# Folding the attention weights of a decoder trunk ahead of its values: more places for raw loads, split weights in idle slots, another order and another pacing

## The chip, the cores and the metric

The kernel runs on one core of one Trainium2 chip. The metric is the device time of one execution in microseconds; the time before is the median of three runs. Beside it there is one profiled execution, whose trace gives the start, the length and the releaser of every instruction on the engines: PE (matrix products, with PEld for the weight loads), DVE (elementwise), ACT (elementwise with scaling and functions), POOL and SP. DMAs are issued from the queues of SP, ACT and POOL.

## The reference

One layer of a decoder trunk over x, 2048 tokens of 1024 channels, all in float32, with 256 memory tokens:

```
h = rmsnorm(x);  q, k, v, g, u = split(h @ w_in)
y = concat(silu(g) * head_rmsnorm(retention(q, k, v)), pool_mixer(u))
x = x + y @ w_out
x = x + cross_attn(rmsnorm(x), rmsnorm(mem), xa_wq, xa_wkv, xa_wo)
x = x + conv_glu_ffn(rmsnorm(x), w_up, conv_w, conv_b, w_down)
out = rmsnorm(x)
```

The cross-attention has four heads of 256 channels. Its scores are (h wq)(mem wk)^T and its output is p (mem wv) wo, so for each head the products wq (mem wk)^T and (mem wv) wo can be made once, before any token is seen. The pooling mixer's per-group weight, its scale and its part of w_out can be multiplied together in the same way.

## The kernel before

**Numbers.** Every float32 operand is split in two parts, a high part rounded to the fast format of PE and a low part with the rest. `split` (line 256 for ACT's high part, line 240 or 248 for DVE's low part) makes both, and `passes` (lines 268 to 270) runs three products per pair: high by high, high by low, low by high. A tile of weights thus goes through a load on SP's queue into a raw place, a split by ACT and DVE into a pair place, and then PE.

**Stages.** The kernel first folds weights (`folded_weights`), then handles the tokens in two halves of 1024: values, head projections with retention and pooling, the mixing with w_out, attention, the output of attention; then the MLP of both halves with a seven-product scheme of block matrices (`rounds`, `run`).

**The folding stage.** `folded_weights` is a generator of 28 units and a closing step, in an order written out by hand. K units (`keys`, 8) and V units (`memory_values`, 8) multiply the memory by a column tile of `wkv`; M units (`score_weights`, one per head, two tiles of `wqT` each) make the score weights and store them in `Md`; O units (`output_weights`, two tiles of `wo` each) make the output weights and store them in `VWd`; W units (`pool_weights`) make `WPd`. Results leave PSUM by ACT into slots of `T` and are stored by DMAs issued from ACT's queue (`keep`, line 519). Between the units the caller, in the main part of the kernel, places other work at fixed unit numbers: eight x tiles (`load_x_wide`, lines 611 to 618: load, split into the slots of X, square, add to a running total), the rope tables (`stored_tables`), the norm of x, the four tiles of value weights (`value_weights`, line 691), and steps of `weight_sums`.

**Places.** `raws` are five places of 128 x 1024 for raw loads: three in `R`, two tiles `S`. In the folding stage two of them hold the memory at first and one holds the running total of x's squares. `wides` are five places for a pair of split parts of 1024: one in `Q`, four in a version of tile `Z` that is replaced by another version after the stage. G holds the split x in its slots 0 to 15 (two per tile of x) and the split memory, keys and values in the slots from 16 on; E has four more slots. `new_raw` and `wide` take the place that was freed longest ago; a load or a split into it waits until its readers are done.

**Order.** The instructions are traced in program order and then put in order by a scheduler with modelled times; calls such as `keep_in_program_order` and `issue_after` hold some of them. Each engine and each queue then runs its own in that order.

**Weight sums.** `weight_sums` prepares block sums for the seven-product schemes (`Ad` for the heads, `Ud` and `Dd` for the MLP) with DMAs from DRAM to DRAM on POOL's queue, some of them accumulating. Each step begins with a tiny ACT instruction (line 942) and a POOL copy (line 943), and issues the next DMAs of up to four jobs; `spacing[0]` says after how many calls the next step comes. There are 52 steps.

**After the fold.** `values` makes the values of the first half with the four tiles of value weights, while `quarter_sums` (line 1510 for its loads) prepares block sums of x, some of them in Z, for the head projections, in which each of 56 items calls `weight_sums`.

Of the kernel before, what the change touches and what calls it, by code (L numbers as in the profile page):

```python
# [8 lines left out]
F32 = mybir.dt.float32  # L9
F32R = mybir.dt.float32r  # L10
I32 = mybir.dt.int32
AF = mybir.ActivationFunctionType
# [8 lines left out]
T = 1024  # L21
SUB = 512
NB = SEQ // T
NS = T // SUB
# [112 lines left out]
def trunk(ctx, tc, xT, memT, pos, w_qkgu, w_v, wkv, wqT, wo, wout_r, wout_p, poolT, w_up, w_dn, vecs, consts, outT):  # L137
# [24 lines left out]
    def new_z(dtype):  # L162
        return Arena(cp.tile([P, 8 * T + 4 * EDGE], dtype, tag="Z", name=nm("Z")), 0, 8, T)

    TT = Arena(cp.tile([P, TEMPS * TW], F32, tag="T", name="T"), 0, TEMPS, TW)
    R = cp.tile([P, 3 * T], F32, tag="R", name="R")
    Q = cp.tile([P, 3 * T], F32R, tag="Q", name="Q")
# [254 lines left out]
    def folded_weights():  # L422

        mp = B.take(4)
# [2 lines left out]
        kk, vv = B.take(4), B.take(4)  # L427
        kp4, vp4 = (r.r.rearrange("p (n i m) -> p n i m", i=2, m=NMEM) for r in (kk, vv))
        own = [prs.take() for _ in range(2)]
        zr = new_z(F32R).t  # L430
        wides = Places([(Q, 0)] + [(zr, 2 * i * T) for i in range(4)], 2 * T)
        memory, first = [raws.take() for _ in range(2)], new_raw()
        for q in range(4):
            to = memory[q // 2].f[:, q % 2 * SUB : (q % 2 + 1) * SUB].rearrange("p (k m) -> p k m", m=NMEM)
# [75 lines left out]
        def memory_values(n):  # L510

            project(KT + n)
            if n % 2:
                split(bank[0].rearrange("p (n m) -> p n m", n=2), vp4[:, n - 1 : n + 1, 0], vp4[:, n - 1 : n + 1, 1])
            if n == KT - 1:
                mp.free()

        def keep(dst, t, n):
            act.dma_start(dst, t.f[:, :SUB].rearrange("p (n c) -> p n c", n=n))
            t.free()  # L520

        def tiles4(d, nh, k):
            return d[4 * nh : 4 * nh + 4, :, k, :].rearrange("n p c -> p n c")
# [1 line left out]
        def score_weights(h):  # L525

            dp = [row_pair(wqT[(2 * h + dt) * P : (2 * h + dt + 1) * P, :]) for dt in range(2)]
            for k2 in range(KT // 2):
                ps = mmps()
                for j in range(2):  # L530
                    for dt in range(2):
                        k = 2 * k2 + j
                        passes(ps[:, j * NMEM : (j + 1) * NMEM], [r[:, k * P : (k + 1) * P] for r in dp[dt]],
                               (kp4[:, 2 * h + dt, 0], kp4[:, 2 * h + dt, 1]), dt == 0, dt == 1)
                t = TT.take()
                for j in range(2):
                    k = 2 * k2 + j
                    act.activation(t.f[:, j * NMEM : (j + 1) * NMEM], ps[:, j * NMEM : (j + 1) * NMEM], AF.Identity, scale=xag[:, k : k + 1])
                keep(Md[h // 2, 2 * k2 : 2 * k2 + 2, :, (h % 2) * NMEM : (h % 2 + 1) * NMEM].rearrange("k p m -> p k m"), t, 2)
            if h == HEADS - 1:  # L540
                kk.free()

        def output_weights(h):

            dp = [row_pair(wo[(2 * h + dt) * P : (2 * h + dt + 1) * P, :]) for dt in range(2)]
            for nh in range(2):
                for mt in range(2):
                    ps = mmps()
                    for dt in range(2):
                        lh = [vp4[:, 2 * h + dt, i, mt * P : (mt + 1) * P] for i in range(2)]  # L550
                        passes(ps, lh, [r[:, nh * SUB : (nh + 1) * SUB] for r in dp[dt]], dt == 0, dt == 1)
                    t = TT.take()
                    act.activation(t.f[:, :SUB], ps, AF.Identity, scale=rn[:, mt : mt + 1])
                    keep(tiles4(VWd, nh, 2 * h + mt), t, 4)
            if h == HEADS - 1:
                vv.free()
# [3 lines left out]
        def pool_weights(g):  # L560

            if g == 0:
                raw = new_raw()
                r3 = raw[:, :SUB].rearrange("p (g c) -> p g c", g=4)
                sp.dma_start(r3, poolT.rearrange("g p c -> p g c"))
                pw = prs.take()
                tt(dve, r3, r3, bcast(pscale, P), ALU.mult)
                split(raw[:, :SUB], pw.r[:, :SUB], pw.r[:, SUB:])
                pool_pair.append(pw)
            pw = pool_pair[0]  # L570
            u = row_pair(wout_p[g])
            for nh in range(2):
                ps = mmps()
                lh = [pw.r[:, i * SUB + g * P : i * SUB + (g + 1) * P] for i in range(2)]
                passes(ps, lh, [r[:, nh * SUB : (nh + 1) * SUB] for r in u], True, True)
                t = TT.take()
                act.activation(t.f[:, :SUB], ps, AF.Copy)
                keep(tiles4(WPd, nh, g), t, 4)
            if g == 3:
                pw.free()  # L580

        def none_left():
            for r in own:
                r.free()

        K, V, M, O, W = keys, memory_values, score_weights, output_weights, pool_weights
        for f, *a in ((K, 0), (K, 1), (K, 2), (K, 3), (K, 4), (K, 5), (M, 0), (K, 6), (K, 7), (M, 1), (V, 0), (V, 1), (M, 2),
                      (V, 2), (V, 3), (M, 3), (V, 4), (V, 5), (O, 0), (V, 6), (V, 7), (O, 1), (W, 0), (W, 1), (O, 2),
                      (W, 2), (W, 3), (O, 3), (none_left,)):
            f(*a)  # L590
            yield

# [87 lines left out]
    def stored_tables(b):  # L680
        for got in rope_tables(b):
            yield
        minus = TT.take()
        act.activation(minus.f[:, :SUB], got[1].f[:, :SUB], AF.Copy, scale=-1.0)
        for i, r in enumerate((*got, minus)):
            sp.dma_start(rope_d[i], r.f[:, :SUB])
            r.free()
# [222 lines left out]
    def weight_sums():  # L910

        jobs = [((w_qkgu[a], w_qkgu[c]), 0, 4, Ad[p]) for p, (a, c) in enumerate(PAIRS)]
        columns = len(jobs)
        jobs += [((w_up[f], w_up[f + NF]), 0, 4, Ud[f]) for f in range(NF)]
        for at, (k0, n) in enumerate(ROUNDS):
            jobs += [((w_dn[2 * j], w_dn[2 * j + 1]), k0, n, Dd[at, j]) for j in range(KT // 2)]

        def sums(w, k0, n, to):
            a11, a12, a21, a22 = (block(w, i // 2, i % 2, k0, n) for i in range(4))
            d = [to[i][:, : n * P] for i in range(4)]  # L920

            def add(at, a):
                pool.dma_start(d[at], a, accum_op=ALU.add, max_dma_last_dim=2048)

            for i, a in ((2, a21), (0, a11), (1, a11), (3, a12)):
                pool.dma_start(d[i], a, max_dma_last_dim=2048)
            yield
            add(2, a22)
            add(0, a21)
            yield  # L930
            add(1, d[2])
            yield
            add(3, d[1])

        live, jobs, at = [], [sums(*j) for j in jobs], 0
        others = len(jobs) - columns
        while jobs or live:
            if jobs and (len(jobs) <= others or at % 2 == 0):
                live.append(jobs.pop(0))
            at += 1  # L940
            here, there = halo[:, at % 32], halo[:, 40]
            tc.keep_in_program_order(act.activation(here, cs_t[:, P : P + 2], AF.Copy))
            turn = pool.tensor_copy(there, here)
            with tc.issue_after(turn.ins):
                live = [g for g in live if next(g, True) is None]
            for _ in range(spacing[0]):
                yield
# [885 lines left out]
    def norm_tables(s_acc, wide=True, late=False):  # L1833

        rn = rows_norm(s_acc)
        rb, last = [], None
        if wide:
            rb = [TT.take() for _ in range(NS)]
            last = spread(rn, [r.f[:, :SUB] for r in rb], late=late)
        return rn, rb, last  # L1840
# [53 lines left out]

        after(2, step)

    under[0], spacing[0] = weight_sums(), 2
    wv, total, tables0 = [], None, stored_tables(0)
    for n, _ in enumerate(folded_weights()):
        if n in (1, 2, 3, 4):  # L1900
            for _ in range(3):
                next(tables0, None)
        if n == 3:
            total = raws.take()
        if n in (4, 6, 8, 10, 12, 14, 16, 18):
            load_x_wide((n - 4) // 2, total)
        if n == 19:
            normed = norm_tables([total], late=True)
        if n in (18, 21):
            wv.append(value_weights(len(wv), 0))  # L1910
        if n in (24, 25):
            wv.append(value_weights(len(wv), 1))
        if n > 19:
            next(under[0], None)
    Z = new_z(F32)
    slow[0], paced[0] = False, True
    for b in range(NB):

        t1, t2 = (B.arenas[0].take(4) for _ in range(2))
# [21 lines left out]
        finish()  # L1941
        rb = normed[1]
        got.append(v)
        parts = [next(heads)]
        mix = got[1]

# [229 lines left out]
```

## Time and profile before

| | us |
|---|---|
| median of 3 runs | 2487.62 (2484.76 to 2488.1) |
| the profiled execution, device time | 2485.65 |
| its span, first to last instruction | 2483.9 |
| PE busy in it | 2413.6 (97%) |
| DVE / ACT / POOL busy | 1740.3 / 1351.4 / 310.8 |
| DMA moved | 514.67 MB, mean 207 GB/s |

The shares of busy time are means over the whole span. The page's slices of 62 us show PE at six and seven tenths in the first three slices and at nine or more in nearly all later ones, and the clock granted to PE at eight tenths in the first three slices. A row "A <- B: total, times, longest" in the waits says that A stood idle until B ended. A row of the timeline has its start, its length, the engine, the source line, the operation with the tiles, and in brackets the idle time before it with its releaser.

### The profile page before, as it was taken

To read this page: it belongs to the slowest core of one execution; us is meant where nothing else is said; L and a number is where in the kernel's file an instruction comes from. 1 tells how busy PE (TensorE), PEld (TensorE's weight loads), DVE (VectorE), ACT (ScalarE), POOL (GpSimd) and SP (SyncE) were. 2 spreads that over 40 slices of the span, in tenths; PEclk is the share of its full clock that TensorE was granted. 3 is DMA by queue.
4 is the path that set the end of the run, shared out by engine and by line. 5 is a ranking of instruction groups with operands and counts; after the bars stand their busy time and mean duration, and the time that the engine had idled before them with its cause. 6 is when DMAs were issued, how large, how long until landed. Compare 5 with 4: busy or idle time off the path is not lost.

```text
span 2483.9 us, 33353 instructions
## 1 busy us (share of the span) xinstructions
PE 2413.6 (97%) x11232; PEld 2013.5 (81%) x11232; DVE 1740.3 (70%) x2869; ACT 1351.4 (54%) x2457; POOL 310.8 (13%) x484
## 2 busy tenths in 40 slices
PE   6779999999999999999999999999999999999998
PEld 6758887888888888888888888888888888888887
DVE  7536677474676776565688777796768688877876
ACT  5544555343454553433555555665555577666664
POOL 0015565464000000000000000020000000000000
PEclk8889999999999999999999999999999999999999
DMA  6699999999543224446558665665556478768952
GB/s 204 220 279 299 288 284 283 314 294 253 192 148 89 77 77 153 128 153 237 187 178 265 218 191 178 198 218 174 168 167 199 142 228 286 259 180 261 360 186 74
DMA packets 272844, 514.67 MB, mean 207 GB/s; under 512 B 29856, under 2 KB 60960, under 8 KB 272672
## 3 DMA queue, kind: packets, MB, share of 16 engines
q1 hardware_dynamic: 210640, 398.11, 49.3%
q0 software_dynamic: 37376, 86.00, 14.4%
q10 hardware_dynamic: 24656, 28.43, 3.3%
q8 instruction: 88, 1.44, 0.2%
q14 instruction: 84, 0.69, 0.1%
HBM read 410.19 MB, written 188.22 MB: 241 GB/s over the span
## 4 chain that ended last, share of the span: by engine, by line
PE 90%; DMA 4%; DVE 3%; ACT 2%; issue 1%; ACTq 0%; SPq 0%; DVEq 0%
PE mm L268 28%; PE mm L269 28%; PE mm L270 28%; DVE Z L240 1%; DMA R<-wqT 1%; PE aux L268 1%; PE aux L270 1%; PE aux L269 1%; PE aux L762 1%; PE aux L747 1%; PE aux L855 1%; PE aux L736 1%; DMA Z<-rope_d 1%; PE aux L764 1%; ACT Z L256 0%
## 5 line engine op out<-in xcount | busy, mean ns | idle before, releaser
L268 PE MATMUL mm<-G,Q 128*128 128x512 f32 (+1 forms) x1574 | 611.7, 389 | 13.8 <-ACT Q L256 11.6
L270 PE MATMUL mm<-G,Q 128*128 128x512 f32 (+1 forms) x1574 | 608.1, 388 | 0.2 <-DVE Q L240 0.2
L269 PE MATMUL mm<-G,Q 128*128 128x512 f32 (+1 forms) x1446 | 562.0, 389 | 0.2 <-DVE G L248 0.2
L269 PE MATMUL mm<-G,E 128*128 128x512 f32 x1052 | 409.1, 389 | 0.0
L268 PE MATMUL mm<-G,E 128*128 128x512 f32 x1052 | 407.4, 389 | 0.0
L270 PE MATMUL mm<-G,E 128*128 128x512 f32 x1052 | 406.9, 389 | 0.0
L268 PEld LDWEIGHTS mm<-G,Q 128*128 128x128 f32 x1574 | 297.5, 189 | 75.6 <-ACT Q L256 12.4
L270 PEld LDWEIGHTS mm<-G,Q 128*128 128x128 f32 x1574 | 296.9, 189 | 59.7 <-DVE Q L240 0.4
L269 PEld LDWEIGHTS mm<-G,Q 128*128 128x128 f32 x1446 | 273.5, 189 | 54.0 <-DVE G L248 0.4
L240 DVE TENSOR_TENSOR Z<-Z,mm 128x512 f32<-128x512 f32 (+1 forms) x322 | 215.7, 674 | 126.2 <-PE mm L270 122.0
L248 DVE SCALAR_TENSOR_TENSOR Z<-Z,vecs 128x1024 f32<-128x1024 f32 x176 | 224.7, 1280 | 49.6 <-ACT Z L1091 46.2
L270 PEld LDWEIGHTS mm<-G,E 128*128 128x128 f32 x1052 | 197.5, 188 | 41.2
L269 PEld LDWEIGHTS mm<-G,E 128*128 128x128 f32 x1052 | 197.5, 188 | 41.0
L268 PEld LDWEIGHTS mm<-G,E 128*128 128x128 f32 x1052 | 197.4, 188 | 41.0
L1028 ACT ACTIVATE E<-R 128x512 fp32r<-128x512 f32 (+1 forms) x165 | 101.6, 616 | 141.0 <-PE mm L269 135.2
L240 DVE TENSOR_TENSOR Q<-R,Q 128x512 fp32r<-128x512 f32 (+1 forms) x158 | 111.2, 705 | 69.1 <-ACT Q L256 42.2
L240 DVE TENSOR_TENSOR T<-T 128x512 f32<-128x512 f32 (+4 forms) x196 | 134.4, 690 | 20.9 <-ACT T L415 10.5
L240 DVE TENSOR_TENSOR G<-T,G 128x512 fp32r<-128x512 f32 x165 | 110.2, 688 | 30.3 <-ACT G L975 15.7
L1091 ACT ACTIVATE Z<-Z,vecs 128x1024 f32<-128x1024 f32 x88 | 109.2, 1242 | 36.0 <-DVE Z L240 35.1
L975 ACT ACTIVATE G<-T 128x512 fp32r<-128x512 f32 x180 | 108.5, 623 | 35.7 <-DMA T<-Gd 27.7
L1028 ACT ACTIVATE E<-S 128x512 fp32r<-128x512 f32 (+1 forms) x107 | 65.9, 616 | 106.6 <-PE mm L269 105.1
L240 DVE TENSOR_TENSOR E<-R,E 128x512 fp32r<-128x512 f32 (+1 forms) x125 | 83.7, 672 | 41.8 <-ACT E L1028 38.6
(348 smaller groups left out, 4160.3 us busy)
## 6 DMA issues: line engine op xcount, KB each, us to landing
T<-Gd SPq DMA_DIRECT2D x168, 256.0 KB, 4.4
Ud<-w_up POOLq DMA_DIRECT2D x132, 256.0 KB, 10.1
Gd<-Z SPq DMA_DIRECT2D x110, 256.0 KB, 2.8
R<-Ud SPq DMA_DIRECT2D x106, 256.0 KB, 2.7
R<-w_up SPq DMA_DIRECT2D x80, 256.0 KB, 3.1
S<-Ud SPq DMA_DIRECT2D x70, 256.0 KB, 2.8
Gd<-T SPq DMA_DIRECT2D x56, 256.0 KB, 3.3
T<-Xd SPq DMA_DIRECT2D x53, 256.0 KB, 4.2
```

Of the source, the lines that this page charges most:

```text
L240: return eng.tensor_tensor(out=out, in0=a, in1=b, op=op)
L248: return dve.scalar_tensor_tensor(out=out, in0=a, scalar=s, in1=b, op0=op0, op1=op1)
L268: pe.matmul(ps, lh, rh, start=start, stop=False, skip_group_check=more)
L269: pe.matmul(ps, lh, rl, start=False, stop=False, skip_group_check=more)
L270: latest[0] = pe.matmul(ps, ll, rh, start=False, stop=stop, skip_group_check=more)
L736: pe.matmul(col(sc, c), self.ch(k, c), self.ch(q, c), start=True, stop=True)
L747: pe.matmul(col(kv, c), col(self.kn.f, c), self.ch(v, c, h * T), start=True, stop=True)
L762: pe.matmul(col(y, c), col(self.pr.f, c), self.ch(v, c, h * T), start=True, stop=self.cur[c] is None)
L764: pe.matmul(col(y, c), self.ch(q, c), self.cur[c], start=False, stop=True)
L975: one = act.activation(hi, x, AF.Copy, scale=-1.0 if i == 2 else 1.0)
L1028: act.activation(p2[:, 0, :w], self.raw[i].f[:, :w], AF.Copy)
L1091: act.activation(self.c[g].f, a[:, 2:], AF.Identity, bias=cb[:, f : f + 1], scale=cw[2][:, f : f + 1])
```

## The change

It touches the folding stage, what surrounds it, and the pacing of the weight sums.

- `raws` has ten places in the stage: the five of before and five in Z, which is now one float32 tile for the whole kernel. The total's place is taken before the memory's.
- `wides` still begins with five places: Q, two pairs in E, two in the slots 12 to 15 of G, where x tiles 6 and 7 come later. After M3 the two in G go and two in the slots of the keys come; after V7 the two in E and the two in the keys' slots go and two in the memory's slots come, so that three are left.
- Results go to six halves at the end of Z in turn, not to slots of T.
- The units' order has each M, O and the W units further behind the K and V units that they need.
- The x tiles come at units 3 to 16 (before 4 to 18), the tables at 7 to 18 (before 1 to 4, three steps each), the norm in two parts at 18 and 20 (before 19), the value weights at 22 to 25 (before 18, 21, 24, 25).
- `weight_sums` is called from unit 8 on with spacing 5 (before from unit 20 with spacing 2), then with 2 in the values as before, with 3 in the heads of the first half (before 2). The heads of the second half keep 4.

The core of the diff:

```
+    Z = new_z(F32)
-        zr = new_z(F32R).t
-        wides = Places([(Q, 0)] + [(zr, 2 * i * T) for i in range(4)], 2 * T)
+        more = B.arenas[1].take(4)
+        wides = Places([(Q, 0)] + [(more.arena.t, i * T) for i in (0, 2)] + [(G, i * T) for i in (12, 14)], 2 * T)
+        def other_places(gone, places):
+            for i in gone:
+                wides.freed.remove(i)
+            for at in places:
+                wides.freed.append(len(wides.one))
+                wides.one.append(Arena(*at[:2], 1, 2 * T))
...
-                mp.free()
+                other_places((1, 2, 5, 6), [(G, mp.arena.base + (mp.first + i) * T) for i in (0, 2)])
+                more.free()
+                kk.free()
+        def result():
+            r = results.take()
+            r.free()
+            return r
...
-                t = TT.take()
+                t = result()
...
-                kk.free()
+                other_places((3, 4), [(G, kk.arena.base + (kk.first + i) * T) for i in (0, 2)])
...
-        for f, *a in ((K, 0), (K, 1), (K, 2), (K, 3), (K, 4), (K, 5), (M, 0), (K, 6), (K, 7), (M, 1), (V, 0), (V, 1), (M, 2),
-                      (V, 2), (V, 3), (M, 3), (V, 4), (V, 5), (O, 0), (V, 6), (V, 7), (O, 1), (W, 0), (W, 1), (O, 2),
-                      (W, 2), (W, 3), (O, 3), (none_left,)):
+        for f, *a in ((K, 0), (K, 1), (K, 2), (K, 3), (K, 4), (M, 0), (K, 5), (K, 6), (M, 1), (K, 7), (V, 0), (M, 2), (V, 1), (V, 2),
+                      (M, 3), (O, 0), (V, 3), (V, 4), (O, 1), (V, 5), (V, 6), (O, 2), (V, 7), (W, 0), (W, 1), (O, 3), (W, 2), (W, 3),
+                      (none_left,)):
...
-    under[0], spacing[0] = weight_sums(), 2
+    under[0], spacing[0] = weight_sums(), 5
+    raws = Places([(R, j * T) for j in range(3)] + [(r, 0) for r in S] + [(Z.t, j * T) for j in range(5)], T)
+    results = Places([(Z.t, 5 * T + j * SUB) for j in range(6)], SUB)
+    wv, total, tables0, x_at = [], raws.take(), stored_tables(0), (3, 4, 6, 7, 9, 10, 15, 16)
     for n, _ in enumerate(folded_weights()):
-        if n in (1, 2, 3, 4):
-            for _ in range(3):
-                next(tables0, None)
-        if n in (4, 6, 8, 10, 12, 14, 16, 18):
-            load_x_wide((n - 4) // 2, total)
+        if n in x_at:
+            load_x_wide(x_at.index(n), total)
+        if n == 18:
+            rn = rows_norm([total])
+        if n == 20:
+            rb = [TT.take() for _ in range(NS)]
+            spread(rn, [r.f[:, :SUB] for r in rb], late=True)
+        if 6 < n < 19:
+            next(tables0, None)
-        if n in (18, 21):
+        if n in (22, 23):
             wv.append(value_weights(len(wv), 0))
-        if n > 19:
+        if n > 7:
             next(under[0], None)
-    Z = new_z(F32)
+    raws = Places([(R, j * T) for j in range(3)] + [(r, 0) for r in S], T)
-    slow[0], paced[0] = False, True
+    slow[0], paced[0], spacing[0] = False, True, 2
...
+        spacing[0] = (3, 4)[b]
```

More of the change, by code (lines that the diff above doesn't have):

```diff
@@ L515, in memory_values @@
             if n == KT - 1:
-                mp.free()
+                other_places((1, 2, 5, 6), [(G, mp.arena.base + (mp.first + i) * T) for i in (0, 2)])
[5 more added lines that the diff above has]
+            return r
         def keep(dst, t, n):
-            act.dma_start(dst, t.f[:, :SUB].rearrange("p (n c) -> p n c", n=n))
-            t.free()
+            act.dma_start(dst, t.f.rearrange("p (n c) -> p n c", n=n))
         def tiles4(d, nh, k):
@@ L551, in output_weights @@
                         passes(ps, lh, [r[:, nh * SUB : (nh + 1) * SUB] for r in dp[dt]], dt == 0, dt == 1)
-                    t = TT.take()
-                    act.activation(t.f[:, :SUB], ps, AF.Identity, scale=rn[:, mt : mt + 1])
+                    t = result()
+                    act.activation(t.f, ps, AF.Identity, scale=rn[:, mt : mt + 1])
                     keep(tiles4(VWd, nh, 2 * h + mt), t, 4)
@@ L575, in pool_weights @@
                 passes(ps, lh, [r[:, nh * SUB : (nh + 1) * SUB] for r in u], True, True)
-                t = TT.take()
-                act.activation(t.f[:, :SUB], ps, AF.Copy)
+                t = result()
+                act.activation(t.f, ps, AF.Copy)
                 keep(tiles4(WPd, nh, g), t, 4)
@@ L582, in none_left @@
         def none_left():
+            mp.free()
             for r in own:
@@ L1895, in later_tiles @@
         after(2, step)
-    under[0], spacing[0] = weight_sums(), 2
-    wv, total, tables0 = [], None, stored_tables(0)
+    under[0], spacing[0] = weight_sums(), 5
+    raws = Places([(R, j * T) for j in range(3)] + [(r, 0) for r in S] + [(Z.t, j * T) for j in range(5)], T)
+    results = Places([(Z.t, 5 * T + j * SUB) for j in range(6)], SUB)
+    wv, total, tables0, x_at = [], raws.take(), stored_tables(0), (3, 4, 6, 7, 9, 10, 15, 16)
     for n, _ in enumerate(folded_weights()):
-        if n in (1, 2, 3, 4):
-            for _ in range(3):
-                next(tables0, None)
-        if n == 3:
-            total = raws.take()
-        if n in (4, 6, 8, 10, 12, 14, 16, 18):
-            load_x_wide((n - 4) // 2, total)
-        if n == 19:
-            normed = norm_tables([total], late=True)
-        if n in (18, 21):
+        if n in x_at:
[5 more added lines that the diff above has]
+            spread(rn, [r.f[:, :SUB] for r in rb], late=True)
+            normed = rn, rb
+        if 6 < n < 19:
+            next(tables0, None)
+        if n in (22, 23):
             wv.append(value_weights(len(wv), 0))
```

## The prediction

> **What bounds the kernel now.** I first read the span and then the busy time by stretch, with the cuts where the stages change.
>
> ```profile
> span 2483.9 us, 33353 instructions
> ```
>
> The columns are busy time of PE, PEld, DVE, ACT and POOL, then granted clock, DMA share and GB/s.
>
> ```profile
> core 0: us, PE busy (x) PEld busy (x) DVE busy (x) ACT busy (x) POOL busy (x), PEclk, DMA share, GB/s
> 0.00:20.00 20.00, 14.73 (x85) 13.13 (x86) 13.93 (x29) 12.35 (x19) 0.20 (x4) 0.94 0.76 236
> 20.00:60.00 40.00, 28.07 (x181) 26.76 (x180) 29.80 (x54) 20.74 (x29) 0.00 (x0) 0.81 0.61 196
> 60.00:100.00 40.00, 25.16 (x192) 24.96 (x192) 22.65 (x21) 24.95 (x36) 0.00 (x0) 0.83 0.66 210
> 100.00:140.00 40.00, 28.24 (x186) 26.76 (x186) 20.82 (x29) 22.33 (x32) 2.85 (x5) 0.80 0.82 262
> 140.00:176.00 36.00, 26.23 (x92) 19.09 (x90) 14.93 (x22) 18.80 (x31) 4.41 (x8) 0.83 0.86 256
> 176.00:220.00 44.00, 43.93 (x182) 36.15 (x183) 21.92 (x34) 20.64 (x45) 21.61 (x36) 0.94 1.07 294
> 220.00:440.00 220.00, 215.42 (x1089) 181.33 (x1088) 155.43 (x319) 111.61 (x278) 122.85 (x192) 0.98 1.08 288
> 440.00:620.00 180.00, 179.45 (x826) 147.53 (x825) 100.68 (x211) 69.31 (x157) 94.49 (x148) 1.00 1.07 286
> ```
>
> From 176 us on PE is busy all but a few us, even with the DMA engines full (share 1.07), so little can be won there. Before 176 us, in the folding of the weights, PE is busy 14.73 + 28.07 + 25.16 + 28.24 + 26.23 = 122.4 of 176 us, at a granted clock near 0.83, and none of the other engines nor the DMA is full over the stage. That is a stage held by waiting. The waits of PE, ACT and SP's queue in 0 to 176 us say on what:
>
> ```profile
> PE mm L268 <- ACT Z L256: 21.6, 4, 11.1
> PE mm L268 <- ACT Q L256: 12.1, 3, 10.4
> ```
> ```profile
> ACT Z L256 <- DMA R<-wqT: 7.4, 4, 3.6
> ACT T L553 <- PE mm L270: 6.9, 2, 4.3
> ACT Q L256 <- DMA R<-wkv: 6.6, 4, 3.4
> ```
> ```profile
> SPq L458 <- DVE Z L240: 26.3, 9, 12.1
> SPq L339 <- DVE Z L240: 23.1, 8, 7.0
> ...
> SPq L339 <- DVE T L245: 6.9, 1, 6.9
> ```
>
> PE waits for the split of the next weights, ACT's split waits for the load, and SP issues the load only when DVE has ended a split, that is when a raw place is free again. The chain of waits shows the loop itself:
>
> ```profile
> 54.26 4.03 DMA R<-wqT
> ...
> 58.38 1.07 ACT Z L256
> ...
> 59.47 1.23 DVE Z L240
> 60.69 1.15 DVE S L240
> ...
> 61.85 4.48 DMA R<-wqT
> ...
> 66.36 1.06 ACT Q L256
> ...
> 67.47 0.58 PE mm L268
> ```
>
> One turn is 61.85 - 54.26 = 7.6 us for a load of 512 KB on the path. The values begin behind the stage's last stop:
>
> ```profile
> 168.92 0.39 PE L268 MATMUL mm<-Q,G 128*128 128x512 f32 x1
> 176.07 0.80 PE L268 MATMUL mm<-G 128*128 128x512 f32 x1 [6.76 <-ACT T L577]
> ```
>
> **The change part by part.** No matrix product, split, load or store is added or removed; places, order and pacing move. So the sum is: how much earlier do the values begin, plus what the moved work costs later.
>
> *Raw places, 5 to 10.* Before, the memory holds two of five at first, then the running total of squares holds one, so four turn. After, the total still holds one and nine turn. About 40 loads go through four places in 17 to 176 us, so a load holds a place for 159 x 4 / 40 = 16 us; nine places at the same holding time would pass them in 40 x 16 / 9 = 71 us. The places then bound nothing, and the next limit decides. I take the floors of 0 to 176 us from the stretches above:
> - PE, busy time times granted clock: 14.73 x 0.94 + 28.07 x 0.81 + 25.16 x 0.83 + 28.24 x 0.80 + 26.23 x 0.83 = 102 us at full clock, 122 us if the clock stays as it is.
> - ACT: 12.35 + 20.74 + 24.95 + 22.33 + 18.80 = 99 us. DVE: 13.93 + 29.80 + 22.65 + 20.82 + 14.93 = 102 us.
> - DMA, share times length: 20 x 0.76 + 40 x 0.61 + 40 x 0.66 + 40 x 0.82 + 36 x 0.86 = 130 us of full share.
>
> So DMA is the highest floor. Two corrections to it:
>
> ```profile
> q1 hardware_dynamic: 10496, 29.97, 53.7%
> q10 hardware_dynamic: 11972, 8.03, 15.0%
> q0 software_dynamic: 891, 2.52, 4.8%
> ```
> ```profile
> 151.23 0.33 SPq L1510 DMA_DIRECT2D R<-xT  x1
> ...
> 162.64 2.25 SPq L1510 DMA_DIRECT2D R<-xT  x2
> ```
>
> (The queues' columns: packets, MB, share of the 16 engines in 0 to 176 us.) Four x loads of L1510 (151.23 to 162.64) are for the next stage: 4 x 0.52 MB at q1's 0.537 x 176 / 29.97 = 3.2 us a MB is 7 us less. The weight sums on POOL's queue take five steps in the fold before (calls 20, 22, 24, 26, 28) and five after (8, 13, 18, 23, 28), 19 transfers of 0.26 MB when all run; about ten had landed by 176, 8.4 us of share, so the rest is at most 8 us more. They nearly cancel: I keep 130. At the mean share of the two best stretches now (0.82 and 0.86, still held by places) the stage would last 130 / 0.84 = 155 us; at the 1.07 of a full queue 121 us plus 4 for the first landing. I take a share of 0.89, above what four places reach and far from full: 146 us. **The term is 176 - 146 = 30 us**, with ends 14 (share 0.80, 162 us) and 46 (share 1.0, 130 us).
>
> The Trainium skill's page "TensorE: Matmul & The Clock Gate", section "HAM oscillation — how this bites in real kernels", says that idle gaps of PE beyond about 3.4 us drop its clock to half; the 0.80 to 0.83 above agree. By it a denser fold runs at full clock and the PE floor is 102 us, without it 122 us; both lie under 146, so the sum stands either way.
>
> *Split weights in x's and the memory's slots.* Five wide places before, five after, two fewer from V7 (call 22) on, when Q and the memory's two are left. The last four units (W1, O3, W2, W3) may then wait for PE's last reading before ACT splits: at most 1.06 + 0.58 us each by the loop's rows, 6.6 us, or nothing where PE runs ahead. I take 0, inside the range. The x tiles 6 and 7 overwrite two of the places (calls 15, 16): their split waits on ACT until PE has read M3's weights, and the splits of V3 stand behind it, but O0 was split before and gives PE 24 products of 512 columns, over 5 us.
>
> *Folds two units behind.* M0 moves from after K5 to after K4, M1 from after K7 to after K6, and so on: each fold needs pairs split a unit or two earlier, so its first product doesn't wait for the evacuation. Worth is inside the 30.
>
> *Results in Z.* Six halves in turn for the 40 stores instead of T slots.
>
> ```profile
> L519 ACTq DMA_DIRECT2D Md<-T x16: 366/366/516, 49.3 to 116.5; - x16
> ...
> DMA to landing us min/median/max: 2.3/4.5/14.2
> ```
>
> Four results a fold and 4.5 us to land fit six places; one of 14.2 us would stop ACT for some us. No term. Z is now one tile: DVE's first writes of the quarter sums into Z wait for the last stores, some 5 us, while PE has 44 us of values before it needs them.
>
> *Tables later.* Some 17 us of DVE work, of which this row is half, moves from calls 1 to 4 to calls 7 to 18.
>
> ```profile
> L248 DVE SCALAR_TENSOR_TENSOR T<-T 128x512 f32<-128x512 f32 x13 | 8.8, 688 | 0.0
> ```
> ```profile
> 20.00:40.00 20.00, 13.41 (x84) 12.71 (x83) 19.25 (x41) 7.44 (x8) 0.00 (x0) 0.80 0.64 212
> ```
>
> In 20 to 40 us DVE is full and PE gets 13.41 of 20: here DVE was the bound, and one load waited 6.9 us behind table work. This is part of the 30. Its last store moves to call 18, some 80 us ahead of the heads that read it.
>
> *Pacing of the sums.* The range of 5 still counts after call 28, so the values get 6 steps and not 8; the heads of the first half one in 3 items and not 2 (19 steps, not 28). About six of 52 steps, those of the down and late up weights, slip into the second half's heads. Before, they run until 593.7:
>
> ```profile
> L942 ACT ACTIVATE halo<-consts x52: 186/188/253, 130.9 to 593.7; 128x2 f32<-128x2 f32 x52
> ```
>
> What takes the load off 220 to 440 us gains nothing while PE is busy 215.42 of 220; what it adds after 620 us meets a DMA at half load. I take 0 (bounds: 2 us gained of the 4.6 idle, 3 lost to late loads).
>
> **Sum:** 2485.65 us of this execution (its span and 1.75 us) less 30 is 2455.7. That execution lies 2.0 under the median of 2487.62; so the median after should be about **2457 us**.
>
> **Rivals.**
> 1. *The DMA is contended early* (chance 0.18). Loads wait in the queues instead of for places. For it: in 176 to 220 us, with sums, loads and stores all active, the share is 1.07 but GB/s only 294; the sums now start at call 8. Against: only five steps of them. Then the share of useful work stays at 0.80, values at 162, gain 14: about 2473. The Trainium skill's page "DMA: Bandwidth & Descriptors", section "SWDGE vs HWDGE vs iDMA", says that each DMA engine serves the software and hardware queues in turn; that speaks for this rival, as the fold's loads would then yield turns to the sums.
> 2. *Near full overlap* (0.10). Share 1.0 or above: values at 130 or sooner, 2441.
> 3. *Slower: ACT stuck in issuing stores* (0.10). The stores are issued from ACT's queue, which also does every split.
>
> ```profile
> 168.41 6.91 ACTq L519 DMA_DIRECT2D WPd<-T  x2
> 175.42 0.60 ACT L577 ACTIVATE T<-mm 128x512 f32<-128x512 f32 x1 [7.57 <-issue]
> ```
>
> At 168 us, with the DMA full, two issues took 6.91 us and PE stood 6.76 us. If the early sums and nine loads in flight fill the queues through the fold, each such stop costs 6.8 us; 30 / 6.8 = 4.4, so from five further stops among 40 stores the gain is gone, and eight cost 54: 2457 + 54 = 2511. Against: before 160 us the stores take 0.37 us each, and most fall there.
> 4. *It doesn't do what it says* (0.07): ACT's fixed order of splits, squares and evacuations, not the places, holds the loads' consumers; ACT waited 4.3 us at once for PE too. Then the fold keeps its length: 2485.
>
> My forecast has 0.55.
>
> **How the numbers follow.** Faster by over 0.2% (5 us, about what a measurement here can tell from none): forecast and rivals 1 and 2, 0.83. Same: rival 4, 0.07. Slower: rival 3, 0.10. The range goes from 2438 (the 46 us end and 3 more) to 2481 (a gain of 6, past rival 1 with the 6.6 us of the wide places); rivals 3 and 4 lie outside, 0.17.
>
> **What would show it.** Right: the first matrix product of the values at 130 to 162 us; SP's waits for DVE's splits (50 us in the two rows quoted) under 15; PE's waits on ACT Z and Q (34 us) under 12, and PE's clock in the fold over 0.9; DVE no longer full in 20 to 40 us; after that PE busy as before, with POOL steps ending near 900 us. Wrong: loads landing in over 8 us with SP no longer waiting (rival 1), ACT stopped in issues before 120 us (rival 3), ACT busy with PE waiting and SP far ahead (rival 4), or new PE waits in the first half's attention.

## The result and the profile after

The changed kernel takes 2456.77 us (median of four runs, 2452.42 to 2459.01) against 2487.86 us before (2484.76 to 2488.48). The ratio is 0.9875 with a 95% interval of 0.9858 to 0.9892: 31 us faster, with 27 to 35 inside the interval. The forecast was 2457 us in a range of 2438 to 2481. The number came out, in part by luck: two of the steps under it did not hold, and the experiments show what they hid.

The profiled execution of the changed kernel is its fastest run (2452.42 us, span 2450.6). First its span, then its stretches with the same cuts as before, where the columns are busy time of PE, PEld, DVE, ACT and POOL, then granted clock, DMA share and GB/s.

```profile
span 2450.6 us, 33403 instructions
```
```profile
0.00:20.00 20.00, 16.74 (x108) 15.33 (x108) 13.46 (x25) 14.81 (x22) 0.20 (x4) 1.00 0.93 333
20.00:60.00 40.00, 23.40 (x159) 22.00 (x159) 35.91 (x63) 24.21 (x33) 0.00 (x0) 0.79 0.58 201
60.00:100.00 40.00, 32.54 (x248) 31.81 (x247) 19.94 (x20) 25.22 (x45) 8.70 (x14) 0.91 1.05 377
100.00:140.00 40.00, 34.79 (x197) 30.09 (x196) 28.30 (x45) 28.58 (x42) 3.16 (x4) 0.96 0.78 222
140.00:176.00 36.00, 35.22 (x153) 28.13 (x152) 17.62 (x25) 17.37 (x29) 8.36 (x15) 1.00 1.02 303
```

PE is busy 142.7 of the first 176 us, before 122.4, and its clock is 0.91 or more except from 20 to 60 us (0.79). The values begin at 149.47 us (before 176.07):

```profile
149.47 0.39 PE L269 MATMUL mm<-G 128*128 128x512 f32 x1
```

In the kernel before, twelve products of the values ran first at half clock (0.43 us apart, later 0.23), and the last eight products of the fold came only behind them (the rows of Q and G):

```profile
176.66 0.63 PE L269 MATMUL mm<-G 128*128 128x512 f32 x1
177.09 0.63 PE L270 MATMUL mm<-G 128*128 128x512 f32 x1
...
182.40 0.39 PE L269 MATMUL mm<-Q,G 128*128 128x512 f32 x1
182.63 0.39 PE L270 MATMUL mm<-Q,G 128*128 128x512 f32 x1
```

So the first product is not the fairest mark. A better one lies behind the fold: the first scores of the retention. The rows are of PE's weight loads of that line in the kernel before and in the changed one; the column after the durations is first and last start.

```profile
L736 PEld LDWEIGHTS aux<-Z x96: 186/192/192, 277.0 to 914.2; 128*128 128x128 f32 x96
```
```profile
L751 PEld LDWEIGHTS aux<-Z x96: 186/192/192, 245.4 to 880.9; 128*128 128x128 f32 x96
```

The lead is 277.0 - 245.4 = 31.6 us there and 33.3 us at the last of them, and the two profiled executions differ by 33.2 us in all (2485.65 - 2452.42): nearly the whole gain is made ahead of 245 us and kept. It is not made in a clean fold. The waits of PE, of SP's queue and of ACT in the changed kernel (totals, times, longest; PE to 160 us, SP and ACT to 140 us):

```profile
PE aux L374 <- DVE Q L241: 11.1, 2, 10.7
PE mm L269 <- ACT E L257: 9.7, 4, 7.0
PE mm L269 <- ACT Q L257: 4.3, 2, 4.1
```
```profile
SPq L340 <- DVE R L241: 15.7, 2, 14.7
```
```profile
ACT Z L552 <- DMA Md<-Z: 7.8, 2, 5.7
```

With the rows of G (1.9 before, 2.6 now) PE's wait for ACT's splits fell from 35.6 us to 16.6, but one of 10.7 us stands at the memory's norm, behind DVE, where the longest was 1.8 before. First the row of before, then three views of the changed kernel:

```profile
PE aux L373 <- DVE Q L240: 2.9, 3, 1.8
```
```profile
20.00:40.00 20.00, 7.79 (x61) 7.18 (x60) 18.42 (x37) 10.34 (x10) 0.00 (x0) 0.83 0.79 281
```
```profile
40.62 0.58 PE L374 MATMUL aux<-Q,ones 128*128 128x256 f32 x1 [10.74 <-DVE Q L241]
```
```profile
L249 DVE SCALAR_TENSOR_TENSOR T<-T 128x512 f32<-128x512 f32 x13 | 8.7, 686 | 0.0
```

The last row is DVE's groups from 20 to 60 us: all 13 of the tables' multiply-adds are there. In the program the tables stand at units 7 to 18, later than before; on the engine they run from 23 to 56 us, before from 12.6 to 40, among the splits and the eleven small steps of the memory's norm, for which PE waits. That the scheduler moved them forward because its model has DVE free there is inferred; that their place in the text does not hold them is shown below (tab_early). The norm itself comes at nearly the same time as before: its first product on PE starts at 40.62 us, before at 39.82. PE now gets there sooner and stands. The places alone bring this wait: it is 11.0 us in the kernel with nothing but the places changed (places_only).

From 60 to 100 us the DMA is full. By queue (packets, MB, share), with the stores of the score weights (count, size, median us to land):

```profile
q1 hardware_dynamic: 3057, 8.68, 55.1%
q10 hardware_dynamic: 3621, 3.49, 25.0%
q0 software_dynamic: 1072, 2.88, 24.5%
...
Md<-Z ACTq DMA_DIRECT2D x12, 256.0 KB, 7.6
```

A quarter of the DMA's time goes to the weight sums, of which three steps run bunched at 68 to 71 us, and the stores take 7.6 us to land in the median, where they took 4.8 in the same stretch before. One store, issued at 74.70 us, takes 16.5 us. ACT then waits for a result place (5.7 us at once, 7.8 in all) and PE for ACT's next split (7.0 us at once).

### The profile page after: what moved, and what is told of

It reads as the page before. It is cut to its first block, busy times and chain, and to the rows that moved or that the text cites. A ratio compares the mean times of both kernels' runs of the same rounds, so it can differ in the third digit from the quotient of the medians.

```text
span 2450.6 us, 33403 instructions
## 1 busy us (share of the span) xinstructions
PE 2401.0 (98%) x11232; PEld 2004.7 (82%) x11232; DVE 1737.4 (71%) x2869; ACT 1349.7 (55%) x2457; POOL 307.3 (13%) x484
## 4 chain that ended last, share of the span: by engine, by line
PE 93%; DMA 3%; DVE 2%; ACT 2%; issue 1%; SPq 0%; ACTq 0%; DVEq 0%
PE mm L269 29%; PE mm L270 29%; PE mm L271 29%; DMA T<-pos 1%; DMA Md<-Z 1%; PE aux L269 1%; PE aux L271 1%; PE aux L270 1%; PE aux L870 1%; PE aux L777 1%; PE aux L762 1%; PE aux L751 1%; PE aux L779 1%; DVE Z L241 1%; ACT G L257 0%
## 5 line engine op out<-in xcount | busy, mean ns | idle before, releaser
L269 PE MATMUL mm<-G,E 128*128 128x512 f32 (+1 forms) x1140 | 433.7, 382 | 9.7 <-ACT E L257 9.7
L271 PE MATMUL mm<-G,E 128*128 128x512 f32 (+1 forms) x1140 | 432.9, 382 | 3.0 <-DVE E L241 3.0
L270 PE MATMUL mm<-G,E 128*128 128x512 f32 (+1 forms) x1140 | 434.8, 382 | 0.0
L269 PEld LDWEIGHTS mm<-G,E 128*128 128x128 f32 x1140 | 215.3, 189 | 51.6 <-ACT E L257 10.5
L271 PEld LDWEIGHTS mm<-G,E 128*128 128x128 f32 x1140 | 215.1, 189 | 45.0 <-DVE E L241 3.9
L270 PEld LDWEIGHTS mm<-G,E 128*128 128x128 f32 x1140 | 215.2, 189 | 41.2
L241 DVE TENSOR_TENSOR Q<-R,Q 128x512 fp32r<-128x512 f32 (+1 forms) x152 | 104.6, 691 | 61.6 <-ACT Q L257 35.1
L1106 ACT ACTIVATE Z<-Z,vecs 128x1024 f32<-128x1024 f32 x88 | 109.1, 1241 | 33.3 <-DVE Z L241 32.4
L241 DVE TENSOR_TENSOR E<-R,E 128x512 fp32r<-128x512 f32 (+2 forms) x126 | 85.0, 676 | 48.4 <-ACT E L1043 39.4
```

The lines of the kernel that those rows point to most:

```text
L241: return eng.tensor_tensor(out=out, in0=a, in1=b, op=op)
L269: pe.matmul(ps, lh, rh, start=start, stop=False, skip_group_check=more)
L270: pe.matmul(ps, lh, rl, start=False, stop=False, skip_group_check=more)
L271: latest[0] = pe.matmul(ps, ll, rh, start=False, stop=stop, skip_group_check=more)
L1106: act.activation(self.c[g].f, a[:, 2:], AF.Identity, bias=cb[:, f : f + 1], scale=cw[2][:, f : f + 1])
```

## The experiments

All twelve ran in four groups, each group beside the kernel before on one chip; the chips differ from group to group, so kernels of different groups are compared by their ratios. The scores column is the first start of the retention's first scores in one profiled execution, which can lie some us off the median (by 4.4 us for the change). The half widths of the ratios are 0.0009 to 0.0027, 2 to 7 us, so two kernels less than some 6 us apart are not told from each other.

| kernel | median us | ratio to before (95%) | first scores us |
|---|---|---|---|
| the change | 2456.77 | 0.9875 (0.9858 to 0.9892) | 245.4 |
| raw5 | 2485.62 | 0.9999 (0.9990 to 1.0008) | 278.9 |
| raw7 | 2459.38 | 0.9894 (0.9871 to 0.9917) | 250.2 |
| places_only | 2462.49 | 0.9908 (0.9884 to 0.9932) | 254.1 |
| order_old | 2461.33 | 0.9900 (0.9881 to 0.9918) | 250.8 |
| pace_old | 2454.74 | 0.9876 (0.9854 to 0.9899) | 247.1 |
| tab_early | 2454.26 | 0.9871 (0.9848 to 0.9894) | 247.2 |
| tab_pin | 2442.94 | 0.9828 (0.9801 to 0.9855) | 236.7 |
| nosums | 2442.19 | 0.9821 (0.9805 to 0.9838) | 235.4 |
| pin_pace | 2437.73 | 0.9807 (0.9782 to 0.9833) | 235.5 |
| pin_res8 | 2438.10 | 0.9813 (0.9799 to 0.9828) | 233.7 |
| pin_sp | 2446.83 | 0.9850 (0.9835 to 0.9865) | 242.8 |
| pin_nosums | 2431.50 | 0.9782 (0.9766 to 0.9798) | 226.8 |

### Five and seven raw places (raw5, raw7)

```
-    raws = ... three in R, two in S, five in Z
+    raws = ... three in R, two in S                  (raw5)
+    raws = ... three in R, two in S, two in Z        (raw7)
```

> The changed kernel with five raw places in the fold (three in R, two in S) and not ten; the total of squares is taken at unit 3 as before; the rest as changed. Theory P (the places are what counted): loads wait for splits again, SP's waits for DVE in the fold go back over 60 us, the values' first evacuation comes near 180 us (160.6 with ten places), about 2478. Rival O (the order of the units and the moved x tiles and tables count): it stays near 165 us, about 2461.

> The changed kernel with seven raw places in the fold (three in R, two in S, two in Z). Theory P1 (a place more always helps, the gain goes with the number of places): about midway between five places (2485.6) and ten (2456.8), 2468 to 2475. Rival P2 (places bind only up to some depth, then DVE and the DMA): within 5 us of ten places, 2455 to 2462.

With five places the gain is gone: ratio 0.9999, some 8 us slower than theory P gave. With seven most of it is back, 0.9894, as rival P2 had it. So nothing of the gain is left without the new raw places, and most of what they bring comes between five and seven; the three further ones are worth 4.7 us by the ratios, which the intervals don't separate from nothing. The waits of SP and the stretch of 20 to 60 us with five places:

```profile
SPq L466 <- DVE E L241: 24.1, 5, 8.7
SPq L340 <- DVE G L241: 15.0, 4, 8.4
```
```profile
20.00:60.00 40.00, 24.43 (x145) 22.77 (x144) 30.11 (x55) 21.42 (x29) 0.00 (x0) 0.70 0.53 175
```

The loads wait for splits again as they did before, and the loop of load, split and load is back in its chain of waits (a load of wqT of 4.34 us, ACT 1.06 us, then PE). Five places lost all 31 us and not only the 22.9 us that the places alone bring in the next run. A likely reason is that the new order and the early x tiles put more loads in flight, which get into each other's way in five places; no run separates this.

### The places alone (places_only)

```
-        for f, *a in ((K, 0), ... (K, 4), (M, 0), (K, 5), ...     order, x tiles, tables, pacing: as changed
+        for f, *a in ((K, 0), ... (K, 5), (M, 0), (K, 6), ...     order, x tiles, tables, pacing: as before
```

> Only the places of the change (ten raw, the wide pairs in E, G and the memory's slots, results in Z); order, x tiles, tables and pacing as before. Theory P: 2455 to 2466, so at least two thirds of the gain of 31. Rival O: 2475 or more.

0.9908: 22.9 us of the 31, as theory P had it. Ten raw places, wide pairs in E, G and the memory's slots, and results in Z bring three quarters of the gain with nothing else moved (by the interval 17 to 29 us). What the wide pairs and the result places do in this without the raw places was not run.

### The order of before, the pacing of before, the tables of before (order_old, pace_old, tab_early)

```
-    x_at = (3, 4, 6, 7, 9, 10, 15, 16), units two behind
+    x_at = (4, 6, 8, 10, 12, 14, 16, 18), units in the order of before      (order_old)
-    spacing 5 from unit 8, heads 3
+    spacing 2 from unit 20, heads 2                                        (pace_old)
-        if 6 < n < 19: one step of the tables
+        if n in (1, 2, 3, 4): three steps of the tables                    (tab_early)
```

> The changed kernel with the units in the order of before and the x tiles at units 4, 6, ... 18 as before (norm at 19 and 20, value weights at 20, 21, 24, 25, as the keys' slots are free there); places, tables and pacing as changed. Theory P: within 5 us of the changed kernel, 2455 to 2462. Rival O: each fold waits for its pairs' evacuation again, eight folds by 2 us, 2470 or more.

> The changed kernel with the pacing of the weight sums as before (called from unit 20, spacing 2 in the fold, the values and the heads). Theory P: the early sums cost something: in the changed kernel three steps run at 68 to 72 us, the DMA is full from 60 to 100 us and ACT waits 7.8 us for result places, PE 7.0; without them about 2450. Rival S (the thinner pacing gives a part of the gain behind the fold, where the lead grows from 26.6 us at the first evacuation of the values to 33.2 us at the last one of the second half): 2460 to 2464.

> The changed kernel with the rope tables at units 1 to 4, three steps each, as before; the rest as changed. Theory T1 (the later place of the tables counts): 3 to 8 us slower than the changed kernel, 2460 to 2465. Rival T2 (the scheduler pulls the tables forward anyway, their first step runs at 23 us in the changed kernel and DVE is full from 20 to 60 us in both): within 3 us, 2454 to 2460.

The old order is 6.2 us behind the change by the ratios, at the edge of what can be told, and inside what theory P gave. The other two are level with it (0.9876 and 0.9871 against 0.9875): neither the new pacing nor the new place of the tables in the text earned anything that can be told. For the tables theory T2 holds: with them at units 1 to 4, DVE is full in 20 to 40 us and PE waits for the memory's norm about as long as in the change (11.7 us at once; the row's other waits are mostly at the norm of x):

```profile
PE aux L374 <- DVE Q L241: 16.8, 5, 11.7
```
```profile
20.00:40.00 20.00, 10.20 (x81) 9.79 (x80) 20.00 (x36) 12.23 (x12) 0.00 (x0) 0.84 0.79 284
```

For the pacing neither theory held: the old one was expected to be 7 us faster or 3 to 7 us slower. It took the bunched sums out of 60 to 100 us, where PE then is busy 39.34 of 40 us, and lost it again at the fold's end, where PE stood 10.2 us at once behind ACT, which was held for 11.81 us in issuing two stores. So the new pacing trades one stop for another.

### Tables held back (tab_pin)

```
-        if 6 < n < 19:
-            next(tables0, None)
+        if 10 < n < 23:
+            with tc.issue_after(x5.ins):        # x5: DVE's addition for the sixth x tile
+                next(tables0, None)
```

> The changed kernel with the tables at units 11 to 22 and each of their DVE instructions held behind the sixth x tile's addition, so that they run some 40 us later. Theory T2: in the changed kernel the tables are what fills DVE from 20 to 60 us (35.9 of 40 us) and what PE's 10.7 us wait at the memory's norm and SP's 14.7 us wait stand behind; with them out of that stretch the wait falls under 4 us and the time by 6 to 12 us, to 2445 to 2451. Rival T3 (DVE's work is only moved and PE waits as long elsewhere in the fold): 2454 to 2459.

11.7 us faster than the change by the ratios, 2 us beyond the range of theory T2. PE's wait at the memory's norm falls from 10.7 us to 1.8, its first product there starts at 30.59 us and not at 40.62, and PE is busy twice as long from 20 to 40 us at the same clock:

```profile
20.00:40.00 20.00, 15.46 (x100) 14.66 (x100) 17.68 (x33) 15.41 (x17) 0.00 (x0) 0.83 0.77 283
```

So the tables did cost the fold time once the places had brought PE forward, and moving them for good was worth 12 us; the change only meant to.

### The weight sums out of the fold (pin_pace, nosums, pin_nosums)

```
-        if n > 7:                         spacing 5
+        if n > 19:                        spacing 2, tables held      (pin_pace)
+        if n > 27:                        spacing 2, tables as changed (nosums), held (pin_nosums)
             next(under[0], None)
```

> The tables held as in the run beside it, and the weight sums called from unit 20 with spacing 2 in the fold as before (heads and later pacing as changed). If the early sums cost the stores their landing (PE's 7.0 us wait at 85 to 92 us) 3 to 7 us under the run with the tables held alone; if the full DMA is only met later, at the end of the fold, within 3 us of it.

> The changed kernel with its tables where they are and no step of the weight sums between the fold's units (the first is called behind the last unit). If the sums' price in the fold is its own, apart from the tables: as much faster than the changed kernel (2456.8) as 2437.7 to 2431.5 with the tables held, plus what the early three steps at 68 us cost, 2444 to 2450. If it only shows once DVE's block of tables is gone, as the fold otherwise waits for DVE: 2453 to 2457.

> The same kernel of 2437.7 us with no step of the weight sums between the fold's units: the first is called behind the last unit (five before). Theory I2 (the sums are what fills the queues at the fold's end): the held issue of 10.74 us goes, 2429 to 2433, unless the heads then wait for their sums. Rival J2 (the loads of x for the quarter sums and the stores fill the queues alone): 2435 to 2440.

Without sums between the units (the first step of five stays, behind the last unit) the changed kernel gains 13.4 us, 2 us beyond the range for a price of their own; with the tables held as well it gains 23.1 us: the two prices nearly add up (11.7 + 13.4 = 25.1). In nosums PE is busy 39.33 of 40 us from 60 to 100 us, the stores there land in 6.3 us and none takes over 7.9, and ACT's wait for the landing of stores to Md is gone. pin_pace is 5.2 us under tab_pin, as it should be if the early sums cost the stores their landing, though the intervals overlap. Its sums come late, and at the fold's end, with the DMA share at 1.04 from 126 to 137 us, two issues of stores held ACT for 10.74 us. The rows are ACT's:

```profile
126.42 10.74 ACTq L534 DMA_DIRECT2D VWd<-Z  x2
137.21 0.69 ACT L567 ACTIVATE Z<-mm,rnm 128x512 f32<-128x512 f32 x1 [10.24 <-issue]
```

In pin_nosums the longest such hold is 3.24 us for two, and the fold runs close to its floors:

```profile
20.00:60.00 40.00, 35.46 (x266) 34.56 (x266) 32.01 (x46) 32.74 (x48) 0.00 (x0) 0.91 0.84 310
60.00:100.00 40.00, 40.00 (x281) 37.21 (x279) 37.44 (x48) 28.74 (x43) 0.00 (x0) 1.00 0.96 317
100.00:140.00 40.00, 34.22 (x145) 26.66 (x145) 23.78 (x45) 27.38 (x46) 4.33 (x9) 0.91 0.90 269
```

PE is full from 60 to 100 us, DVE at 37 of 40, the DMA at 0.96. The sums that move out of the fold run at the end of the list, in the second half's heads (until 838 us), and PE meets no new wait for them up to 700 us beyond 1.9 us. At 2431.50 us it lies in the range of theory I2: without the sums the held issue is gone.

### Stores on SP's queue, more result places (pin_sp, pin_res8)

```
-            act.dma_start(dst, ...)
+            sp.dma_start(dst, ...)              # VWd and WPd      (pin_sp)
-    raws: five places in Z, results: six
+    raws: four places in Z, results: eight                         (pin_res8)
```

> The kernel with the held tables and the sums from unit 20 (2437.7 us), with the stores of the output and pooling weights issued from SP's queue and not from ACT's. There two issues at 126 us took 10.74 us of ACT and PE waited 9.3. Theory I (an issue that is held up by full queues stops its engine, and ACT is the engine that PE waits for): PE's wait for ACT at the fold's end falls under 3 us and the time by 5 to 9 us, to 2429 to 2433. Rival J (SP is held up in its place and the loads behind it, so PE waits as long for a load): 2436 to 2441.

> The same kernel of 2437.7 us with eight result places and nine raw ones in Z, where it has six and ten. If results wait for places (ACT waited 7.8 us for a landing in the changed kernel, 1.9 us in this one): 1 to 3 us faster; if a place less for loads counts more: 1 to 3 us slower; most likely within 2 us, 2436 to 2440.

pin_sp goes Rival J's way and beyond: 0.9850 against pin_pace's 0.9807, about 10 us slower. Theory I's first half holds, as PE's longest wait for ACT at the fold's end falls from 9.3 us to 2.3. But SP's queue is held in ACT's place, and the next stage's loads of x stand between and behind the stores:

```profile
130.62 6.94 SPq L534 DMA_DIRECT2D VWd<-Z  x3
137.66 1.11 SPq L1527 DMA_DIRECT2D R<-xT  x1
...
139.36 6.41 SPq L534 DMA_DIRECT2D WPd<-Z  x4
```

PE pays for it later, with one stop that ends at 200 us, among the head projections:

```profile
PE mm L271 <- DVE Q L241: 8.4, 1, 8.4
```

The chain that leads there goes back over two slow landings (10.77 us of a rope table, 12.01 us of a weight tile) to a stop of DVE at 148 us. There it stood 10.4 us before it wrote a block sum of x into Z, where the results lie too: the last store of WPd from Z took 13.75 us to land. PE also waits longer for the norm of x, 8.0 us at once where it was 2.0 in pin_pace. How the 10 us divide among these is not shown.

The Trainium skill's page "DMA: Bandwidth & Descriptors", section "Issuing engines are not separate DMA queues", says that DMAs of all issuers run on the same engines and that another issuer only saves the time of issuing, which is usually small beside the transfer. The traces agree that another issuer doesn't help; the time of issuing was not small, with 10.74 us for two issues on ACT and 6.94 us for three on SP. pin_res8 is level with pin_pace: the result places don't bind there.

## Why the prediction was right, point by point

**Where the stage was held.** Right. Raw places were the first limit of the fold: without the new ones nothing is gained (raw5), with the new places and nothing else three quarters (places_only). The working took the limit as gone with nine places in turn; it is nearly gone with seven places, six in turn (raw7).

**The term of 30 us.** The first product of the values came at 149.47 us, not 146, at a mean DMA share of 0.83 to there (20 x 0.93 + 40 x 0.58 + 40 x 1.05 + 40 x 0.78 + 9.5 x 1.02 = 125, over 149.5), not 0.89; the work of 130 was sized well. By the prediction's own mark the gain is 176.07 - 149.47 = 26.6 us, not 30. The lead at the first scores is 31.6 us, 5.0 more: in the kernel before, eight products of the fold (8 x 0.23 = 1.8 us) and the half clock of twelve products of the values (12 x 0.20 = 2.4 us) lay behind the mark. The sum left these out, and that they make up for the missing 3.4 us is luck.

**"Some 17 us of DVE work moves from calls 1 to 4 to calls 7 to 18 ... This is part of the 30."** This step failed. The work did not move past 56 us, DVE was still busy 18.42 of 20 us from 20 to 40 us, and putting it back costs nothing (tab_early). What the step should have asked is what holds the instructions back: nothing did, and the order on the engine is the scheduler's. Held for good it is worth 11.7 us more.

**"They nearly cancel: I keep 130" for the weight sums.** The volume was right and the price wrong. The four steps of sums between the units cost about 13 us (nosums), 10.0 of them ahead of the first scores, by the landing of the stores and ACT's wait for places, not by their 8 us of DMA time. This is the mechanism of rival 1, which had 0.18, at work inside the likeliest case: some loads came late too (three of wo took 8.5 us to land in the median, 5.7 in nosums), though the stop of PE stood behind a store.

**"One of 14.2 us would stop ACT for some us. No term."** It came: one store took 16.5 us to land, and ACT stood 5.7 us for its place. With the sums away none from 60 to 100 us took over 7.9 us.

**The pacing behind the fold at 0.** Right: the lead is 31.6 us at the first scores and 33.3 at the last, and pace_old, which has the old pacing in the fold too, is level.

**Order and x tiles, "inside the 30".** Their part is 6.2 us by the ratios (order_old), at the edge of the noise.

**Rival 3, ACT stuck in issuing stores.** In the changed kernel the longest hold is 2.70 us, so it did not decide; its mechanism is real. In the five kernels with the sums from unit 20 at spacing 2 and the stores on ACT (before, places_only, pace_old, pin_pace, pin_res8) the longest hold is 6.9 to 11.8 us, in the other eight with the stores on ACT 2.6 to 6.0.

**The signs.** The values' start, PE's clock in most stretches and the end of the sums (837 us, before 594, forecast near 900) were as foretold. SP's waits for DVE did not go under 15 us (one alone is 14.7), PE's for ACT not under 12 (16.6), and DVE was still nearly full in 20 to 40 us. SP's waits were a poor sign: all its rows behind DVE to 145 us add up to 94 us before, 78 after, 86 in raw5 and 84 in pin_nosums, so they hardly tell the slowest fold from the fastest. PE's waits for ACT to 176 us do: 37, 18, 40 and 4 us. Two misses of the size of 12 us each stood within the chosen share of 0.89 against the possible 1.0: with both taken away the first scores come 50.2 us earlier than before (277.0 - 226.8), near the end of 46 us that rival 2 was given.

## What to carry to other kernels

When an engine waits for a split, the split for a load and the load for a place, count the places in turn and try the next few: here five to seven was most of the step, and ten showed the next limits. Read the waits of the engine that bounds the stage; a queue that issues loads waits for places in a slow stage and in a fast one. A stage that is freed of one wait should be read again at once: the new longest waits (an elementwise block in the way of a small chain, background DMA in the way of stores) were worth 23 us, as much again as the places alone. Work that is to run later must be held by an edge to an instruction, not by its place in the text, where a scheduler orders the queues.

## What the runs showed of the hardware that was not expected

A DMA issue is not a fixed cost: one issue on ACT's queue took 9.11 us in places_only and two took 10.74 us in pin_pace, where one takes 0.37 us otherwise, and the engine does nothing meanwhile. Moving them to another issuer moves the stop. Full DMA engines alone don't bring it: from 60 to 100 us of the changed kernel, at a share of 1.05, all twelve stores took 0.37 to 0.39 us to issue. The issues held longest were all stores to VWd or WPd, whose packets are half the size of those to Md (ACT's queue moved 3.49 MB in 3621 packets from 60 to 100 us of the changed kernel, 2.79 MB in 5619 from 100 to 140); whether that is the reason no run tells.

Background traffic shows in the slowest transfers more than in the median. From 60 to 100 us the stores to Md landed in 4.8 us in the median before, at 210 GB/s; in 6.3 us without sums (nosums, 353 GB/s, the slowest 7.9); and in 7.6 us with the sums at 24.5% of the DMA's time (377 GB/s, the slowest 16.5). So about half of the longer landing is there without the sums, with the loads packed closer; the sums add the rest, and the slow one for which ACT stood.
